# Retention heads that start their own rotary and scores early, an earlier write of token sums, and exchanged PSUM banks

## The chip, the core and the metric

The kernel runs on one core of a Trainium2 chip. A core has TensorE (PE, matmuls, with its weight loads shown as PEld), VectorE (DVE), ScalarE (ACT), GpSimd (POOL), and SyncE (SP), which here only issues transfers. Transfers between the chip's main memory (DRAM here) and on-chip SBUF run on 16 DMA engines, and are issued from the queues of SP, ACT and POOL. Matmuls write to PSUM, which has a few banks; VectorE and ScalarE read it out. The metric is the device time in microseconds (us). A comparison gives the median of several runs.

## What is computed

A trunk of two layers on 256 tokens of width 2048, in float32: gated linear attention (GLA, 4 heads), then retention (8 heads), each with a SiLU gate, and a final RMS norm. The retention layer, cut:

```python
proj = h @ w_in                               # q, k: 8 heads x 256; v, gate: 8 heads x 512
q, k = apply_rotary(q, cos, sin), apply_rotary(k, cos, sin)
scores = einsum(q, k) * dmat                  # causal, decays with a factor per head
o = scores @ v                                # (state between chunks of 64 in the reference)
o = ((o - mu) * rsqrt(var + EPS)) * gn_g + gn_b      # per head
return (o * silu(gate)) @ w_out
```

## The kernel before

Each weight matrix is read in blocks of 128 x 1024 float32 (512 KB, two slices of 128 rows by 512 columns). For each block ScalarE writes `hi` (line 283) and VectorE `lo = raw - hi` (line 284), and TensorE makes three products, hi with the high and the low part of the activations, and lo with the high part. So each block costs one ScalarE and one VectorE pass, and splits run up to three blocks ahead of TensorE (`LOOK = 3`; `hi` and `lo` have four buffers, the raw blocks eight).

For a pair of column groups (values "v" and gates "g" of a head, or two column groups of an output projection) the kernel uses products of sums of blocks (P1 to P8 in the code): some blocks are loaded a second time with an accumulating transfer on GpSimd's queue (line 292), some are added on VectorE (line 278), and the activations' token sums (`make_sums`) stand as a tensor `sums` on chip. The sums are needed again by heads 4 to 7, so `keep_sums` (line 449, GpSimd's queue) writes them to DRAM and `reload_sums` brings them back.

Order of the work: GLA heads 0 and 1, output projection "ga"; GLA heads 2 and 3, output projection "gb"; retention heads 0 to 3, output projection "ra"; heads 4 to 7, output projection "rb", and a tail. `out_pair` makes a pair of output columns: products into four banks B, A, C, V1; after the product with the fourth sum, ScalarE copies bank A to `u3`, and the blocks of `direct(lhs, (B, A), 4)` then overwrite A. `join` adds a bank into the residual on VectorE, `whole` takes its square sum on ScalarE (`sqj`).

A retention head (`ret_head`) works through a written list of tokens. Heads 1, 2, 3, 5, 6, 7 are "mixed":

```python
MIXED = "q0 q1 P1 q2 q3 q4 z P5 q5 P6 q6 q7 P2 P3 v4 v5 v6 P7 v7 g4 g5 P8 g6 g7"
```

Here q0 to q7 are the blocks of the query/key projection, P1 to P8 the products, v and g the direct blocks of values and gates. Its first half ends with q7; I call the rest, from P2, its second half. Heads 0 and 4 do all q blocks first.

The attention itself is a generator, `ret_tasks`: 1 multiply by cos (`ra`), load `dm`; 2 multiply by sin (`rb`), load `gg` and `gb`; 3 combine; 4 split into `rqs`, `rks`, score matmuls (`rs`); 5 multiply by `dm`, split scores (`rsc`); 6 output matmuls (`ro`), mean and variance; 7 multiply by `gg`; 8 the reciprocal root; 9 add `gb`; 10 multiply by the gate (`rsg`); 11 and 12 transposes (`rot_tp`) and their evacuation to `ogt`, the activations of the output projection. `step()` runs one stage. Before the change a head's stages are queued at its token P8, two run at g6 and g7, and the others in the first half of the next head; at token P2 (v5 in heads 0 and 4) what is left is run out. After heads 3 and 7, the stages run within the first blocks of "ra" and "rb" (`out_steps`), whose first two column groups leave the last two row blocks to the end (`CUT = 6`), since these need the last head's `ogt`.

A planner in the framework orders the instructions on each engine from this program; `keep` holds the written order of an engine's marked instructions, and `tc.high_priority()` lets an instruction go ahead of others. Four PSUM tiles, acc0 to acc3, serve the projections, two ("lev") hold half of q and k, two ("mis") scores, outputs and transposes. `slots` gives the order in which projections take acc0 to acc3; `acc(..., which=[n])` names one.

Of the kernel before, what the change touches and what calls it, by code (L numbers as in the profile page):

```python
# [14 lines left out]
AF = mybir.ActivationFunctionType  # L15
ALU = mybir.AluOpType

P = 128
SEQ = 256
# [142 lines left out]
def kernel(  # L162
# [17 lines left out]
    nc = tc.nc  # L180
# [20 lines left out]
    keep = tc.keep_in_program_order  # L201
# [9 lines left out]
    slots = deque(range(4))  # L211
# [4 lines left out]
    def acc(n, name, shape=(P, GW), which=None):  # L216
        out = []
        for i in range(n):
            k = slots[0] if which is None else which[i]
            if which is None:  # L220
                slots.rotate(-1)
            out.append(acc_p.tile(list(shape), F32, tag=f"acc{k}", name=f"{name}{i}"))
        return out
# [83 lines left out]
    def drain_side():  # L307
        while side:
            advance()

    def next_weights():
        i = state["sub"]
        while emitted["sub"] <= min(i + LOOK, len(subs) - 1):
            emit_split()
        state["sub"] += 1
        return splits.pop(i)
# [71 lines left out]
    def three(ps, xh, xl, hi, lo, q, stop):  # L388
        start, again = id(ps) not in begun, {"skip_group_check": id(ps) in closed}
        begun.add(id(ps))  # L390
        mm(ps, xh, hi[:, q, :], start=start, stop=False, **again)  # L391
        mm(ps, xh, lo[:, q, :], start=False, stop=False, **again)  # L392
        mm(ps, xl, hi[:, q, :], start=False, stop=stop, **again)  # L393
        if stop:
            closed.add(id(ps))

    def product(ps, left, stop=False):
        for j in range(2):
            hi, lo = next_weights()
            for q in range(SUB):  # L400
                k = j * SUB + q
                three(ps, left(k, 0), left(k, 1), hi, lo, q, stop and k == QK - 1)
# [170 lines left out]
    def square_sum(t, c):  # L573
        junk = sg_p.tile([P, GW], F32, tag="sg", name="sqj")
        nc.scalar.activation(
            junk, cur["resid"][:, t, c * GW : (c + 1) * GW], AF.Square, accum_out=ssum[:, t, c : c + 1]
        )
# [363 lines left out]
    def out_transposes(c):  # L941
        return transpose_out(
            lambda t, j: cur["resid"][:, t, c * GW + j * P : c * GW + (j + 1) * P],
            4 * c,
            S_RN + 4 * c,
            xhl,
            f"xt2_{c}",
        )

    def out_pair(c, first, name):  # L950
        lhs, s = ogt, cur["s"]
        B, A, C, V1 = acc(4, f"{name}e{c}_ps", which=list(slots))
        slots.rotate(-2)
        P5 = lev_p.tile([P, GW], F32, tag="lev", name=f"{name}e{c}_p5")
        plain = lambda kt0, t: lambda k, a: lhs[:, kt0 + k, a, t * P : (t + 1) * P]
        summed = lambda i: lambda k, a: s[i][:, k, a, :]
        u3 = t4_p.tile([P, 2, GW], F32, tag="t4", name=f"{name}e{c}_u3")[:, 0, :]

        def join(col, t, src, op=ALU.add):
            dst = cur["resid"][:, t, col * GW : (col + 1) * GW]  # L960
            if op == ALU.add:
                keep(nc.vector.tensor_tensor(dst, src, dst, ALU.add))
            else:
                keep(nc.vector.tensor_tensor(dst, dst, src, ALU.subtract))

        def whole(col, t):
            if not first:
                square_sum(t, col)

        late = deque() if first else deque([out_transposes(c)])  # L970

        def turn():
            advance()
            if late:
                next(late[0], None)

        g = c + 1
        product(A, plain(0, 0), stop=True)
        advance()
        direct(lhs, (C, V1), 4)  # L980
        join(g, 0, A)
        advance()
        product(C, summed(0))
        advance()
        direct(lhs, (C, V1), 5)
        drain_side()
        product(P5, summed(1), stop=True)
        direct(lhs, (C, V1), 6)
        for t in range(2):
            join(c, t, P5)  # L990
        product(A, summed(2), stop=True)
        product(B, plain(4, 0))
        join(c, 0, A, ALU.subtract)
        direct(lhs, (C, V1), 7, stop=True)
        product(A, summed(3), stop=True)
        join(c, 0, C)
        whole(c, 0)
        keep(nc.scalar.activation(u3, A, AF.Copy))
        direct(lhs, (B, A), 4)
        join(c, 1, u3, ALU.subtract)  # L1000
        join(c, 1, V1)
        whole(c, 1)
        direct(lhs, (B, A), 5)
        turn()
        product(A, plain(4, 1))
        turn()
        direct(lhs, (B, A), 6)
        turn()
        direct(lhs, (B, A), 7, stop=True)
        join(g, 0, B)  # L1010
        whole(g, 0)
        join(g, 1, A)
        whole(g, 1)
        if not first:
            for _ in late[0]:
                pass
            tasks.append(out_transposes(g))
        begun.clear()
        closed.clear()
# [208 lines left out]
    tasks = deque()  # L1228

    def step(n=1):  # L1230
        for _ in range(n):
            if tasks:
                try:
                    next(tasks[0])
                except StopIteration:
                    tasks.popleft()

    def ret_head(h):
        lhs = xhl
        mixed = h % 4 != 0  # L1240
        q_ps = [acc(1, f"rqk{h}_ps{c}", (P, 2, SEQ), [c + 2])[0] for c in range(2)]
        q_ps += [lev_p.tile([P, 2, SEQ], F32, tag="lev", name=f"rqk{h}_ps{c}") for c in (2, 3)]
        if not mixed:
            q_ps = q_ps[2:] + q_ps[:2]
        r, r2 = r2_[:, 0, :], r2_[:, 1, :]
        box = {}

        def qk_done():
            if h == 0:
                token_norm(r2_, "n2")  # L1250
                nc.vector.tensor_tensor(r2_[:, 1, :], r2_[:, 0, :], r2_[:, 0, :], ALU.mult)
            qk = t4_p.tile([P, 4, SEQ], F32, tag="qk", name=f"rqk{h}", bufs=1)
            tmp = t4_p.tile([P, 4, SEQ], F32, tag="t4", name=f"rqk{h}_h2")
            for c in range(4):
                nc.scalar.activation(tmp[:, c, :], q_ps[c][:, 1, :], AF.Copy)
                nc.vector.tensor_tensor(qk[:, c, :], q_ps[c][:, 0, :], tmp[:, c, :], ALU.add)
            box["qk"] = qk

        def q_step(j):
            step_w(lhs, q_ps, j)  # L1260
            if j == NSUB - 1:
                qk_done()

        def tile_of(key, pool_, shape, dtype, name):
            def get():
                if key not in box:
                    box[key] = pool_.tile(shape, dtype, tag=key, name=name)
                return box[key]

            return get  # L1270

        v = tile_of("v", v_p, [P, 2, 2, GW], F32R, f"rv{h}")
        sg = tile_of("sg", sg_p, [P, 2, GW], F32, f"rsg{h}")
        o = tile_of("o", o_p, [P, 2, GW], F32, f"re{h}")
        order = ret_order(h)
        toks = [x for x in order.split() if x != "z"]
        drain = toks.index("P2" if mixed else "v5")

        def turn(tok):
            n = toks.index(tok)  # L1280
            if n == drain:
                while tasks:
                    step()
            elif n < drain and tok not in ("q7", "P3"):
                step()
            elif tok == "P8":
                tasks.append(ret_tasks(h, box["qk"], r, r2, box))
            elif tok in ("g6", "g7"):
                step()

        def banks(n):
            if n not in box:
                box[n] = acc(1, f"re{h}_ps{n}", which=[n])[0]
            return box[n]

        values_and_gates(lhs, order, banks, v, sg, o, r, r2, turn, q_step)
# [69 lines left out]
        closed.clear()  # L1366

    def out_steps(i, j):
        step(2 if i == 0 and j < 3 else 1)

    for h in range(2):
        gla_head(h)
    slots = deque((2, 3, 0, 1))
    out_half(True, False, "ga", joint=JOINT["ao", 0])
    slots = deque((2, 3, 0, 1))
# [1 line left out]
    for h in range(2, 4):  # L1377
        gla_head(h)
    get_resid("gb_resid")
    slots = deque((0, 1, 2, 3))  # L1380
    out_half(False, False, "gb", joint=JOINT["ao", 1])
    put_resid("resid_g")
    if True:
        tasks.append(make_sums(xhl, "sums", sums_in_rs))
        for h in range(4):
            if h == 3:
                keep_sums("sums")
            ret_head(h)
    slots = deque((2, 3, 0, 1))
    tasks.append(make_sums(ogt, "rsum", sums_in_v))  # L1390
    out_half(True, False, "ra", CUT, out_steps, JOINT["ro", 0])
    put_resid("resid_r")
# [4 lines left out]
    slots = deque((2, 3, 0, 1))  # L1397
# [102 lines left out]
```

## Time and profile before

| | us |
|---|---|
| median of 3 runs | 1388.12 |
| lowest and highest | 1386.97, 1389.71 |
| the profiled execution | 1389.8 |
| its span, first to last instruction | 1387.9 |
| mean granted TensorE clock | 0.997 |

The page of the profile gives each engine's busy time and share of the span. Further views give the busy time by stretches of the span, the instructions in order of time with the idle time before each and what ended it, groups of equal instructions, and the transfers. In them L364 is line 364 of the kernel, `re_ps` a retention head's value and gate banks, `rqk_ps` its q and k, `gb_ps`, `gbe_ps`, `ra_ps`, `rb_ps` banks of the output projections. An instruction is busy from start to end; waits on semaphores are idle time.

### The profile page before, as it was taken

The page shows a single profiled execution, that of the slowest core. Times are in us where ns is not written, and L with a number is a line of the kernel's source. Part 1 is how long each engine was busy: PE and PEld are TensorE (multiplying, and loading weights), DVE is VectorE, ACT ScalarE, POOL GpSimd, SP SyncE. Part 2 cuts the span into 40 slices and gives each one's busy share as a digit, 9 for nine tenths or more (in the row PEclk, how much of TensorE's full clock was granted, in tenths as well). Part 3 has the DMA queues.
Part 4 walks back from the last instruction along what each step waited for, and adds up shares of the span by engine and source line. Part 5 has one row for each costly group of instructions (what it writes and reads, how often), then busy time and mean ns, then how long its engine had stood idle before and what let it go on. Part 6 is the DMA issues. An engine that isn't in the chain of part 4 may idle for free.

```text
span 1387.9 us, 18436 instructions
## 1 busy us (share of the span) xinstructions
PE 1370.5 (99%) x6632; PEld 1149.2 (83%) x6632; DVE 1078.2 (78%) x1497; ACT 837.4 (60%) x1104; POOL 131.9 (10%) x188
## 2 busy tenths in 40 slices
PE   9999999999999999999999999999999999999997
PEld 7888888888888888887888887887888888888887
DVE  6686795987878887779788877888767888888773
ACT  6576656655567747565666665654546666666552
POOL 1003020110021021001011010100101101010000
PEclk9999999999999999999999999999999999999999
DMA  9755556789659658758797878796698796969661
GB/s 354 247 181 167 172 170 182 165 248 349 193 152 275 184 174 219 277 166 258 227 288 200 257 228 267 197 326 201 158 377 224 235 275 174 283 174 336 205 191 62
DMA packets 83932, 312.94 MB, mean 225 GB/s; under 512 B 9713, under 2 KB 10737, under 8 KB 82561
## 3 DMA queue, kind: packets, MB, share of 16 engines
q1 hardware_dynamic: 67344, 242.64, 50.4%
q0 software_dynamic: 15056, 61.74, 22.0%
q10 hardware_dynamic: 1440, 7.38, 1.4%
q8 instruction: 52, 0.85, 0.2%
q14 instruction: 40, 0.32, 0.1%
HBM read 301.24 MB, written 10.49 MB: 225 GB/s over the span
## 4 chain that ended last, share of the span: by engine, by line
PE 51%; DMA 1%; DVE 1%; ACT 0%; issue 0%; DVEq 0%; ACTq 0%
PE rqk_ps L364 8%; PE re_ps L391 8%; PE re_ps L393 8%; PE re_ps L392 8%; PE rqk_ps L365 4%; PE rb_ps L321 2%; PE rb_ps L323 2%; PE rb_ps L322 2%; PE ra_ps L321 1%; PE ra_ps L322 1%; PE ra_ps L323 1%; PE rae_ps L392 1%; PE rae_ps L393 1%; PE rae_ps L391 1%; DMA raw<-in_w_all 1%; PE tail_ps L323 1%
## 5 line engine op out<-in xcount | busy, mean ns | idle before, releaser
L284 DVE TENSOR_TENSOR lo<-raw,hi 128x1024 fp32r<-128x1024 f32 (+1 forms) x557 | 673.7, 1221 | 231.3 <-ACT hi L283 226.2
L283 ACT ACTIVATE hi<-raw 128x1024 fp32r<-128x1024 f32 (+1 forms) x557 | 584.0, 1056 | 394.7 <-DMA raw<-in_w_all 52.5
L364 PE MATMUL rqk_ps<-xhl,hi 128*128 128x512 f32 x480 | 166.7, 397 | 0.0
L392 PE MATMUL re_ps<-lo,xhl 128*128 128x512 f32 x352 | 137.8, 391 | 0.1
L393 PE MATMUL re_ps<-hi,xhl 128*128 128x512 f32 x352 | 137.8, 392 | 0.0
L391 PE MATMUL re_ps<-hi,xhl 128*128 128x512 f32 x352 | 130.7, 392 | 0.4 <-ACT hi L283 0.4
L365 PE MATMUL rqk_ps<-xhl,lo 128*128 128x256 f32 x480 | 127.8, 281 | 0.0
L292 POOL DMA_DIRECT2D raw<-in_w_all x84 | 72.8, 868 | 570.0 <-DVE lo L284 291.3
L364 PEld LDWEIGHTS rqk_ps<-xhl,hi 128*128 128x128 f32 x480 | 89.4, 188 | 18.6
L365 PEld LDWEIGHTS rqk_ps<-xhl,lo 128*128 128x128 f32 x480 | 88.7, 189 | 3.0
L392 PEld LDWEIGHTS re_ps<-lo,xhl 128*128 128x128 f32 x352 | 66.5, 189 | 14.1 <-DVE lo L284 0.6
L391 PEld LDWEIGHTS re_ps<-hi,xhl 128*128 128x128 f32 x352 | 66.2, 188 | 14.3 <-ACT hi L283 0.8
L393 PEld LDWEIGHTS re_ps<-hi,xhl 128*128 128x128 f32 x352 | 66.4, 189 | 13.8
L364 PE MATMUL gqk_ps<-xhl,hi 128*128 128x512 f32 x216 | 76.5, 398 | 0.0
L322 PE MATMUL gg_ps<-lo,xhl 128*128 128x512 f32 x192 | 75.4, 393 | 0.0
L322 PE MATMUL gv_ps<-lo,xhl 128*128 128x512 f32 x192 | 75.2, 392 | 0.0
L321 PE MATMUL gv_ps<-hi,xhl 128*128 128x512 f32 x192 | 75.1, 393 | 0.0
L323 PE MATMUL gv_ps<-hi,xhl 128*128 128x512 f32 x192 | 75.0, 391 | 0.0
L323 PE MATMUL gg_ps<-hi,xhl 128*128 128x512 f32 x192 | 75.0, 390 | 0.0
L321 PE MATMUL gg_ps<-hi,xhl 128*128 128x512 f32 x192 | 74.8, 391 | 0.0
L365 PE MATMUL gqk_ps<-xhl,lo 128*128 128x256 f32 x216 | 59.0, 280 | 0.0
L801 POOL TENSOR_TENSOR s<-s,m 128x64 f32<-128x64 f32 x56 | 36.1, 677 | 233.4 <-DVE m L792 224.1
(407 smaller groups left out, 2683.5 us busy)
## 6 DMA issues: line engine op xcount, KB each, us to landing
raw<-in_w_all SPq DMA_DIRECT2D x451, 512.0 KB, 4.9
raw<-in_w_all POOLq DMA_DIRECT2D x84, 512.0 KB, 7.0
resid<-in_x_n SPq DMA_DIRECT2D x2, 1024.0 KB, 9.0
gg<-in_gn_g POOLq DMA_DIRECT2D x8, 256.0 KB, 5.6
resid_x<-resid ACTq DMA_DIRECT2D x1, 2048.0 KB, 8.3
gb<-in_gn_b POOLq DMA_DIRECT2D x8, 256.0 KB, 3.8
gb_resid<-resid_x POOLq DMA_DIRECT2D x1, 2048.0 KB, 11.7
resid_g<-gb_resid ACTq DMA_DIRECT2D x1, 2048.0 KB, 9.3
```

The lines of the kernel that those rows point to most:

```text
L283: a = nc.scalar.activation(hi[:, sl], src[:, sl], AF.Copy)
L284: b = nc.vector.tensor_tensor(lo[:, sl], src[:, sl], hi[:, sl].bitcast(F32), ALU.subtract)
L292: nc.gpsimd.dma_start(raws[n], block(key), accum_op=ALU.add)
L321: mm(ps, xh, hi[:, q, :], start=kt == 0, stop=False)
L322: mm(ps, xh, lo[:, q, :], start=False, stop=False)
L323: mm(ps, xl, hi[:, q, :], start=False, stop=kt == NKT - 1)
L364: mm(ps[c], wh, rhs[:, kt, :, :], start=kt == 0, stop=False)
L365: mm(ps[c][:, 0, :], wl, rhs[:, kt, 0, :], start=False, stop=False)
L391: mm(ps, xh, hi[:, q, :], start=start, stop=False, **again)
L392: mm(ps, xh, lo[:, q, :], start=False, stop=False, **again)
L393: mm(ps, xl, hi[:, q, :], start=False, stop=stop, **again)
L801: nc.gpsimd.tensor_tensor(dst, dst, side_of(m[:, li, :], z), ALU.add)
```

## The change

Four edits. In `out_pair` the copy `u3` is written ahead of the joins and marked with high priority. In `ret_head` a table `at` exchanges acc0, acc1 with acc2, acc3 in heads 0 to 3, and the `slots` of "gb" and "ra" are exchanged to match. In mixed heads the stages are queued at P2, once the tasks of the head before are run out, and one stage runs at each of P3, v4, v5, v6, v7, P8, g6 and g7; the others run in the next head's first half, where heads 0 and 4 now also run one at P3, and `out_steps` runs one a block. `keep_sums` is called ahead of head 1 in place of head 3.

```diff
@@ out_pair
         product(A, summed(3), stop=True)
+        with tc.high_priority():
+            keep(nc.scalar.activation(u3, A, AF.Copy))
         join(c, 0, C)
         whole(c, 0)
-        keep(nc.scalar.activation(u3, A, AF.Copy))
         direct(lhs, (B, A), 4)
@@ ret_head
-        q_ps = [acc(1, f"rqk{h}_ps{c}", (P, 2, SEQ), [c + 2])[0] for c in range(2)]
+        at = (2, 3, 0, 1) if h < 4 else (0, 1, 2, 3)
+        q_ps = [acc(1, f"rqk{h}_ps{c}", (P, 2, SEQ), [at[c + 2]])[0] for c in range(2)]
...
             if n == drain:
                 while tasks:
                     step()
-            elif n < drain and tok not in ("q7", "P3"):
-                step()
+                if mixed:
+                    tasks.append(ret_tasks(h, box["qk"], r, r2, box))
+            elif n < drain:
+                if tok != "q7":
+                    step()
+            elif mixed:
+                if tok not in ("P7", "g4", "g5"):
+                    step()
             elif tok == "P8":
                 tasks.append(ret_tasks(h, box["qk"], r, r2, box))
             elif tok in ("g6", "g7"):
...
-                box[n] = acc(1, f"re{h}_ps{n}", which=[n])[0]
+                box[n] = acc(1, f"re{h}_ps{n}", which=[at[n]])[0]
@@ out_steps
-        step(2 if i == 0 and j < 3 else 1)
+        step()
@@ the order of the work
-    slots = deque((0, 1, 2, 3))
+    slots = deque((2, 3, 0, 1))
     out_half(False, False, "gb", joint=JOINT["ao", 1])
...
         for h in range(4):
-            if h == 3:
+            if h == 1:
                 keep_sums("sums")
             ret_head(h)
-    slots = deque((2, 3, 0, 1))
+    slots = deque((0, 1, 2, 3))
```

## The prediction

> **What bounds the kernel now.** I read the page first (busy time by engine), then cut the span into stretches around every pause of TensorE, then compared the four retention heads that run the same program, and last looked up in the timeline what ended each pause.
>
> ```profile
> PE 1370.5 (99%) x6632; PEld 1149.2 (83%) x6632; DVE 1078.2 (78%) x1497; ACT 837.4 (60%) x1104; POOL 131.9 (10%) x188
> ```
>
> TensorE is busy for 1370.5 of 1387.9 us. The change takes no matmul away, so all it can win lies in the 17.4 us in which TensorE is idle, or in time at a lower clock. The stretches below hold (start and end:length, busy time of TensorE, weight loads, VectorE, ScalarE, GpSimd, the granted clock, the DMA engines' busy share, GB/s):
>
> ```profile
> 0.00:8.00 8.00, 4.83 (x11) 3.12 (x12) 2.57 (x5) 3.49 (x6) 2.42 (x12) 1.00 0.74 228
> 566.00:569.00 3.00, 2.54 (x12) 1.83 (x11) 2.86 (x8) 1.49 (x2) 0.00 (x0) 1.00 1.03 423
> 644.00:648.00 4.00, 2.87 (x13) 1.74 (x12) 4.00 (x5) 2.00 (x4) 0.00 (x0) 1.00 1.01 412
> 835.00:846.00 11.00, 9.32 (x35) 6.71 (x34) 6.32 (x6) 6.04 (x7) 0.00 (x0) 0.91 0.89 302
> 966.00:969.00 3.00, 1.20 (x10) 0.92 (x9) 2.71 (x5) 3.00 (x5) 0.00 (x0) 1.00 0.84 280
> 1322.00:1325.00 3.00, 2.24 (x15) 1.75 (x14) 1.62 (x2) 2.03 (x3) 0.00 (x0) 1.00 0.75 220
> 1376.00:1388.00 12.00, 3.89 (x33) 3.69 (x31) 3.64 (x12) 2.54 (x8) 0.00 (x0) 0.81 0.23 87
> ```
>
> Idle TensorE time, row by row (length less busy): 3.17 at the start, 0.46, 1.13, 1.68, 1.80, 0.76, and 8.11 at the end; together 17.11. What is left is one wait, at 323 us (a timeline row: start, duration, engine, line, what; in brackets the idle time before it and what ended that):
>
> ```profile
> 323.08 0.50 PE L392 MATMUL gae_ps<-lo,ogt 128*128 128x512 f32 x1 [0.43 <-DVE lo L284]
> ```
>
> Start and end are not touched. The five pauses in between are, and each lies at one part of the change: the entry into the output projection "gb" (567 us), the copy u3 in its column pair (645), head 2 (836 to 844), and the two waits for the last head's transposes (967 and 1323).
>
> ```profile
> 720.78:788.21 67.43, 67.43 (x337) 56.96 (x335) 55.63 (x76) 42.18 (x56) 6.90 (x9) 1.00 0.82 233
> 788.21:860.01 71.80, 70.12 (x336) 58.07 (x335) 55.91 (x76) 42.25 (x56) 7.43 (x10) 0.98 0.82 245
> 860.01:927.62 67.61, 67.61 (x336) 57.05 (x335) 55.87 (x76) 42.38 (x56) 7.49 (x10) 1.00 0.82 249
> 1148.71:1216.31 67.60, 67.60 (x336) 57.04 (x335) 56.01 (x76) 42.63 (x56) 6.91 (x9) 1.00 0.80 229
> ```
>
> These are heads 1, 2, 3 and 6, each from its first q block to the next head's. Three take 67.4 to 67.6 us with TensorE busy throughout; head 2 takes 71.80, so it loses 4.2 us: 1.68 of pause, the rest around it at a granted clock of 0.98 over the head.
>
> **The change part by part.** All sums are against the profiled execution: 1389.8 us, span 1387.9, so 1.9 us lie around the span. It is 1.7 us above the median of the three timed runs (1388.12); I carry a difference found here over to that median.
>
> *Token sums written at the second head (keep_sums at h == 1 in place of 3).* What head 2 has and the others lack is this write (its second row: KB, and us from issue to landing):
>
> ```profile
> 813.75 0.56 POOL L449 DMA_DIRECT2D sums_kept<-sums  x1
> sums_kept<-sums POOLq DMA_DIRECT2D x1, 2048.0 KB, 8.5
> 820.00:838.00 18.00, 17.87 (x90) 14.79 (x90) 13.48 (x23) 10.07 (x14) 2.27 (x3) 1.00 1.03 270
> 842.16 0.51 PE L391 MATMUL re_ps<-hi,sums 128*128 128x512 f32 x1 [1.10 <-ACT hi L283]
> 844.00:848.00 4.00, 4.00 (x12) 3.15 (x11) 3.62 (x5) 2.49 (x4) 0.00 (x0) 0.57 0.81 279
> 848.00:852.00 4.00, 4.00 (x19) 3.33 (x18) 4.00 (x6) 2.52 (x4) 0.00 (x0) 1.00 0.89 312
> ```
>
> It is issued at 813.75, just ahead of two accumulating weight loads. For 18 us after 820 the DMA engines are full (1.03); the weight tiles come late, ScalarE's split "hi" comes late, and TensorE pauses. Right behind, the clock is 0.57 for 4 us: 12 matmuls start in place of 19 (both stretches count as busy). Seven starts at 4.00/19 = 0.21 us make some 1.5 us, so pauses and clock give 3.2 of the 4.2; the rest is the slower restart after each wait. In the built order of the changed kernel the write stands on the GpSimd queue in head 0, behind the two accumulating loads of P1 and ahead of the next two (raw225, raw226). It waits only for the sums:
>
> ```profile
> 686.32 1.29 DVE L443 TENSOR_TENSOR sums<-sums_f,sums 128x512 fp32r<-128x512 f32 x2
> 686.00:690.00 4.00, 4.00 (x20) 3.30 (x19) 3.68 (x5) 3.57 (x5) 0.00 (x0) 1.00 0.04 8
> 690.00:694.00 4.00, 4.00 (x19) 3.34 (x18) 3.87 (x5) 1.77 (x3) 0.77 (x1) 1.00 0.45 133
> 693.23 0.87 POOL L292 DMA_DIRECT2D raw<-in_w_all  x1 [13.01 <-DVE raw L278]
> ```
>
> The sums are ready at 687.6 and the DMA engines are nearly idle until 690 (0.04), half idle until 694. At 8.5 us from issue to landing the write would end near 696, 3 us past the next accumulating load's issue. The bounds of the gain are 4.2 (head 2 becomes like 1, 3 and 6, no new cost) and 0 (the same collision, moved). I take 4.0, since most of the write falls into the hole, and 0.2 for the rest. [...]
>
> On the clock the rows come first: the one dip in mid-span (0.57) follows directly on a 1.10 us wait, while the 1.80 us pause at 967 left the clock at 1.00. I count the dip as caused by head 2's late loads. [...]
>
> *The u3 copy under high priority, ahead of the joins.*
>
> ```profile
> 645.93 0.63 ACT L575 ACTIVATE sqj<-gb_resid 128x512 f32<-128x512 f32 x1 [1.13 <-DVE gb_resid L962]
> 646.56 0.58 ACT L998 ACTIVATE gbe_u<-gbe_ps 128x512 f32<-128x512 f32 x1
> 646.04 0.41 PE L679 MATMUL xt_tp<-ident,gb_resid 128*128 128x128 f32 x2 [0.39 <-DVE gb_resid L962]
> 647.19 0.50 PE L391 MATMUL gbe_ps<-hi,ogt 128*128 128x512 f32 x1 [0.74 <-ACT gbe_u L998]
> ```
>
> ScalarE stands idle for 1.13 us in front of the square sum, which waits for VectorE's join; u3 is queued behind it, and TensorE waits for u3 before it may overwrite bank A. In the changed order u3 stands ahead of split 251 and the square sum, so it can run in that idle 1.13 us; the transposes that waited 0.39 stand later on TensorE. Queued behind u3's own wait (for product A) are only split 251 and the square sum, neither due sooner. So 1.13 at most. What is late next is VectorE: the stretch from 644 to 648 has it busy for 4.00 of 4.00. I take 0.8, between 0 and 1.13. In the other three pairs the only pause is the 0.43 at 323 us, for a split: nothing.
>
> *PSUM banks exchanged.*
>
> ```profile
> 567.93 0.47 PE L321 MATMUL gb_ps<-hi,ogt 128*128 128x512 f32 x1 [0.46 <-DVE hr_nw L476]
> ```
>
> The first gb group used banks 0 and 1, the gate banks of the group before, which are read out last; it now uses 2 and 3, the value banks, read out earlier. Gain 0.46 (0 to 0.46). Heads 0 to 3 and "ra" are relabelled together, and before head 4 there was no pause to win: 0.
>
> *Mixed heads start their tasks in their own second half.* Eight of a head's steps (rotary, scores, output product) leave the next head's first half, so at the end of heads 3 and 7 five steps are left in place of twelve.
>
> ```profile
> 968.61 0.50 PE L321 MATMUL ra_ps<-hi,ogt 128*128 128x512 f32 x1 [1.80 <-ACT ogt L686]
> 1323.89 0.50 PE L321 MATMUL rb_ps<-hi,ogt 128*128 128x512 f32 x1 [0.76 <-ACT ogt L686]
> ```
>
> Both waits are for ogt, the evacuation of the last head's transposes. In the changed order these stand some five 12-matmul blocks ahead of the first use in ra, seven in rb, where now they stand right in front of it. Gain 1.80 + 0.76 = 2.56 (0 only if the transposes are not moved). One step a block in out_steps in place of two is enough: five tasks and six steps of "rsum" fit the twelve early blocks.
>
> The price lies in the second halves, on VectorE. A second half in the trace, and what is added to it or taken from it (groups: count | busy us, mean ns of one | idle before):
>
> ```profile
> 1185.00:1216.30 31.30, 31.30 (x143) 25.96 (x142) 26.02 (x30) 19.24 (x22) 2.24 (x3) 1.00 0.90 282
> L1154 DVE TENSOR_TENSOR ra<-rqk,trig 128x1024 f32<-128x1024 f32 x3 | 3.7, 1218 | 0.0
> L1154 DVE TENSOR_TENSOR ro<-ro,rsg 128x512 f32<-128x512 f32 x4 | 2.7, 682 | 0.0
> L1154 DVE TENSOR_TENSOR ra<-ra,rb 128x512 f32<-128x512 f32 x4 | 2.6, 685 | 0.0
> L1154 DVE TENSOR_TENSOR rb<-rqk,trig 128x512 f32<-128x512 f32 x4 | 2.6, 684 | 0.0
> L687 DVE TENSOR_TENSOR ogt<-rot_tp,ogt 128x512 fp32r<-128x512 f32 x4 | 2.6, 680 | 0.0
> L1154 DVE TENSOR_TENSOR rqs<-ra,rqs 128x512 fp32r<-128x512 f32 x2 | 1.4, 686 | 0.0
> L1154 DVE TENSOR_TENSOR rs<-rs,dm 128x384 f32<-128x384 f32 x2 | 1.1, 549 | 0.0
> ```
>
> Added up to the score split: 1.22 + 2 x 0.68 + 2 x 0.69 + 0.69 for rqs, at most the same for the smaller rks, and 2 x 0.55 for the scores and their split: 6.4 us. Gone to the first half: 2 x 0.68 + 2 x 0.68 = 2.7. So 26.0 + 6.4 - 2.7 = 29.7 of VectorE in 31.3 us of TensorE, which itself grows by the moved score and output matmuls. That fits, at 95% or less; in heads 1 and 5, where the previous head's tail still stays in the second half, nothing is taken away: 32.4, about equal to the longer half. VectorE's new wait (the score multiply, for the score matmuls of v7) has the splits of P8 queued behind it, but the value sums ahead of it wait for v7 already. On the GpSimd queue dm and gg move ahead of accumulating loads; their buffers are free by then in the built order (gb's last reader stands ahead of P6's split), so they hold nothing up. I put 0.3 us on the whole, between 0 and 2 us for each of six heads, the size of the largest pause seen.
>
> Sum: 4.0 + 0.8 + 0.46 + 2.56 - 0.3 = 7.5 us; a slow restart came with each pause too (the matmul after it takes 0.47 to 0.51 us), some 0.1 each at the four smaller ones: 7.9. The profiled execution would be 1381.9, the median 1388.12 - 7.9 = 1380.2 us.
>
> **The rivals.** *The collision moves.* The write is late or slow, P5 to P7 of head 0 starve as head 2 did, and 4.0 to 4.2 us are lost again there. For it: accumulating loads follow at 693.23 and share the engines. Against: the 0.04 and 0.45 of DMA share. Time: 1380.2 + 4.1 = 1384.3. [...]
>
> *The dip of the clock stays.* It has another cause than the late loads and comes again at full cost, 1.5 us; for it, the longer pause at 967 had none. Time: 1381.7. [...]
>
> *VectorE becomes the bound of the second halves (slower).* The split of a weight tile comes late behind the eight steps, once in each of six mixed heads. It decides from where the added work no longer fits, 31.3 us against 29.7; with a pause of 2 us a head (1.80 is the largest seen) it costs 12 us: 1380.2 + 12 = 1392. Against: 26.0 us busy now, and matmuls that move along.
>
> *Little is won.* The pauses are refilled by later ones since VectorE (78%) and the weight loads (0.8 to 0.9 of DMA share in the heads) have no room to run ahead; 1.5 us a head in four heads takes 6.0 of the 7.9: 1386.2, inside 0.2% (2.8 us), which is about what a measurement of this kernel can tell from no change.
>
> **How the numbers follow.** My forecast has 0.68, the dip that stays 0.04, the moved collision 0.14, little won 0.06, VectorE-bound 0.08. Faster: 0.86; same: 0.06; slower: 0.08. The range reaches down to all five pauses gone with nothing paid (4.2 + 1.13 + 0.46 + 2.56 + 0.5 = 8.85) with the fastest run of the three as its base (1386.97 - 8.85 = 1378.1, rounded to 1378.0), and up to the moved collision with 0.3 more for the splits, 1384.6.
>
> **What would show it.** Right: head 2 as long as head 3; no TensorE pause over 0.5 us at gb's entry, at u3, at the ends of heads 3 and 7; the granted clock at 1.00 in mid-span; sums_kept landing by 696. Wrong: pauses on hi or lo in head 0 after 690 (the collision moved), or on lo in P8 to g7 of heads 1, 2, 5 and 6 (VectorE-bound).

## The result, and the profile after

| | before | after |
|---|---|---|
| median of 6 runs, us | 1388.9 | 1379.8 |
| lowest to highest | 1386.97 to 1389.71 | 1378.94 to 1382.26 |
| profiled execution, us | 1389.8 | 1379.47 |
| its span | 1387.9 | 1377.6 |

The ratio after to before is 0.9939, with a 95% interval from 0.9926 to 0.9952: 6.7 to 10.3 us less, 8.5 in the middle (the two medians lie 9.1 apart). The forecast was 7.9 us less, at 1380.2.

From the page of the changed kernel, the span, the busy time by engine and the chain of waits by engine:

```profile
span 1377.6 us, 18438 instructions
PE 1366.5 (99%) x6632; PEld 1148.5 (83%) x6632; DVE 1079.1 (78%) x1497; ACT 836.0 (61%) x1104; POOL 131.8 (10%) x188
PE 99%; DMA 0%; DVE 0%; ACT 0%; DVEq 0%; issue 0%; SPq 0%
```

TensorE's idle time fell from 17.4 to 11.1 us (span less busy time), and its busy time by 4.0, with the same 6632 matmuls. The chain that ended last is TensorE from end to end. The stretches below hold the places of the five pauses (columns as in the prediction; the first and the last row are the start and the end of the span):

```profile
0.00:8.00 8.00, 4.88 (x11) 3.17 (x12) 2.53 (x5) 3.15 (x5) 2.41 (x12) 1.00 0.73 231
560.00:570.00 10.00, 10.00 (x46) 8.29 (x45) 8.90 (x22) 6.95 (x10) 0.00 (x0) 1.00 1.01 414
640.00:650.00 10.00, 10.00 (x46) 7.96 (x45) 8.55 (x9) 7.35 (x9) 0.00 (x0) 1.00 0.98 380
786.00:856.00 70.00, 70.00 (x347) 58.79 (x346) 56.17 (x76) 43.78 (x62) 6.93 (x9) 1.00 0.80 222
955.00:965.00 10.00, 10.00 (x46) 8.29 (x45) 5.23 (x6) 3.50 (x4) 0.00 (x0) 1.00 0.65 203
1318.00:1326.00 8.00, 8.00 (x37) 6.61 (x36) 7.07 (x9) 4.56 (x8) 0.54 (x1) 1.00 0.66 209
1366.00:1377.60 11.60, 3.57 (x30) 3.37 (x29) 3.64 (x12) 2.55 (x8) 0.00 (x0) 0.82 0.24 90
```

In every row between the start and the end the second number equals the first: TensorE has no pause left at gb's entry, at u3, in head 2, or in front of ra's and rb's last blocks. What is left is 3.12 us at the start and 8.03 at the end, 11.15 together, which is all of its idle time. In mid-span the granted clock is 1.00, head 2's place included.

What moved can be seen on ScalarE and GpSimd (timeline rows of the changed kernel; the fourth is the first matmul that needs the activations of the third):

```profile
642.27 0.57 ACT L997 ACTIVATE gbe_u<-gbe_ps 128x512 f32<-128x512 f32 x1
684.82 0.56 POOL L449 DMA_DIRECT2D sums_kept<-sums  x1 [7.64 <-DVE sums L443]
946.40 1.09 ACT L686 ACTIVATE ogt<-rot_tp 128x512 fp32r<-128x512 f32 x2 [0.18 <-PE rot_tp L679]
959.49 0.39 PE L321 MATMUL ra_ps<-hi,ogt 128*128 128x512 f32 x1
```

The copy u3 stands ahead of the square sum (which starts at 644.44), with no wait in front of it. ogt's evacuation ends at 947.5, twelve microseconds before its first use, where before it stood right in front of it. The write of the sums is issued at 684.82, as soon as the sums are ready; what it meets is shown by its row among the transfers (KB, us from issue to landing) and then by four stretches:

```profile
sums_kept<-sums POOLq DMA_DIRECT2D x1, 2048.0 KB, 9.5
```

```profile
684.00:688.00 4.00, 4.00 (x20) 3.30 (x19) 3.69 (x4) 3.28 (x4) 0.56 (x1) 1.00 0.64 262
688.00:692.00 4.00, 4.00 (x19) 3.34 (x18) 4.00 (x5) 1.64 (x3) 0.86 (x1) 1.00 0.93 293
692.00:696.00 4.00, 4.00 (x20) 3.30 (x19) 3.47 (x3) 2.88 (x4) 2.56 (x3) 1.00 1.04 267
700.00:710.00 10.00, 10.00 (x46) 8.28 (x45) 7.76 (x8) 5.24 (x8) 0.00 (x0) 1.00 1.04 304
```

It lands at 694.3. Everything ahead of it runs 3 us earlier than before: the sums are ready at 684.5, where they were at 687.6. So most of the write falls into the stretch that before had a share of 0.04 and 0.45, and its last 3 us lie behind it. The engines are full from 692 on (1.04), as they were in head 2 of the kernel before, but no split comes so late that TensorE stops.

The time thus came from two sources in the trace: 6.3 us of idle TensorE in mid-span, and 4.0 us of slow busy time (the half-clock stretch, and the restarts after each pause, both measured below). Their 10.3 us are more than the 8.5 of the comparison; a reason is found below.

### The profile page after: what moved, and what is told of

Same layout as the page of the kernel before. It is cut to its first block, busy times and chain, and to the rows that moved or that the text cites. A ratio compares the mean times of both kernels' runs of the same rounds, so it can differ in the third digit from the quotient of the medians.

```text
span 1377.6 us, 18438 instructions
## 1 busy us (share of the span) xinstructions
PE 1366.5 (99%) x6632; PEld 1148.5 (83%) x6632; DVE 1079.1 (78%) x1497; ACT 836.0 (61%) x1104; POOL 131.8 (10%) x188
## 4 chain that ended last, share of the span: by engine, by line
PE 99%; DMA 0%; DVE 0%; ACT 0%; DVEq 0%; issue 0%; SPq 0%
PE rqk_ps L364 8%; PE re_ps L392 8%; PE re_ps L391 8%; PE re_ps L393 8%; PE rqk_ps L365 4%; PE gqk_ps L364 4%; PE gg_ps L322 3%; PE gv_ps L321 3%; PE gv_ps L322 3%; PE gv_ps L323 3%; PE gg_ps L323 3%; PE gg_ps L321 3%; PE ge_ps L392 2%; PE ge_ps L393 2%; PE ge_ps L391 2%; PE gae_ps L391 2%
## 5 line engine op out<-in xcount | busy, mean ns | idle before, releaser
L364 PE MATMUL rqk_ps<-xhl,hi 128*128 128x512 f32 x480 | 162.8, 397 | 0.0
L365 PE MATMUL rqk_ps<-xhl,lo 128*128 128x256 f32 x480 | 122.3, 280 | 0.0
```

The source lines that it names most:

```text
L364: mm(ps[c], wh, rhs[:, kt, :, :], start=kt == 0, stop=False)
L365: mm(ps[c][:, 0, :], wl, rhs[:, kt, 0, :], start=False, stop=False)
```

## The experiments

Four kernels take one part of the change each, four undo one part each, one doubles the moved write, one puts it at another head, and two repeat profiles for the clock. The theory was the prediction's: each pause has its own cause in one of the edits, and the write costs nothing as long as it lies in the hole after head 0's sums. The rival was that pauses only move.

**One part alone.** *The write alone:*

```diff
-            if h == 3:
+            if h == 1:
                 keep_sums("sums")
```

> The kernel before with keep_sums at head 1 in place of head 3, nothing else. Theory (the write collided with head 2's loads, and the hole in head 0 hides it): head 2 falls from 71.8 to about 67.6 us, no dip of the clock in mid-span, head 0 unchanged, the total about 4 us less (0.3%). Rival (the collision moves): head 0 is about 4 us longer and the total the same. Rival (the dip of the clock has another cause): head 2 loses its pauses, but some stretch of 3 to 4 us still runs at half clock, the total about 2.5 us less.

Measured: ratio 0.9979 (0.9971 to 0.9988), 2.9 us less; span 1385.7. Head 2 is mended, with full clock (first row), yet TensorE slows down at another place: behind the wait for ogt at ra, which in the kernel before had left the clock at full (the stretches first, then the timeline row of that wait).

```profile
788.21:855.83 67.62, 67.62 (x336) 57.04 (x335) 55.81 (x76) 42.54 (x56) 6.89 (x9) 1.00 0.81 228
966.00:970.00 4.00, 4.00 (x12) 3.15 (x12) 0.54 (x1) 0.00 (x0) 0.00 (x0) 0.62 0.27 103
```

```profile
964.45 0.50 PE L321 MATMUL ra_ps<-hi,ogt 128*128 128x512 f32 x1 [1.79 <-ACT ogt L686]
```

So the pauses of head 2 do belong to the write, but the dip does not.

*The tasks alone* (the two hunks of `ret_head`'s task list, and `out_steps`):

```diff
+                if mixed:
+                    tasks.append(ret_tasks(h, box["qk"], r, r2, box))
...
-        step(2 if i == 0 and j < 3 else 1)
+        step()
```

> The kernel before with the mixed heads' stages begun in their own second half and one stage a block in out_steps, nothing else. Theory: the waits for ogt (1.80 at 967, 0.76 at 1323) go, 2.6 to 3 us; and keep_sums, written as before ahead of head 3, is issued later than before, in head 3's first half, where the moved stages have changed the load: if the collision depends on where the write meets the accumulating loads, head 2 loses its 4.2 us and head 3 may gain some of it. So 3 to 7 us less in total. Rival (VectorE becomes the bound of second halves): pauses on lo in P8 to g7 of heads 1, 2, 5, 6, heads 5 and 6 longer than 67.6 by up to 2 us each, total as before or longer.

Measured: 0.9981 (0.9972 to 0.9990), 2.6 us less; span 1382.9. Both waits for ogt are gone. The planner then moved the write of the sums, still called at head 3, from head 2 into head 3, and it paused TensorE there instead (0.86 at 883.9). Pauses of 0.18 and 0.75 on `lo` came at 922 and 924, which further runs show not to be the write's. There was no dip in mid-span, and with 3.5 us its idle time in mid-span is the least of the four (4.9 with the write alone, 5.3 with u3, 5.8 with the banks), so its span is the shortest.

*u3 alone:*

```diff
+        with tc.high_priority():
+            keep(nc.scalar.activation(u3, A, AF.Copy))
         join(c, 0, C)
         whole(c, 0)
-        keep(nc.scalar.activation(u3, A, AF.Copy))
```

> The kernel before with the copy u3 ahead of the joins under high priority, nothing else. Theory: the pause at 645 (0.39 and 0.74) goes, and with VectorE full there 0.8 to 1.5 us less in total; all other pauses stay. Rival (VectorE is late next): the same time comes back as waits on lo within the next four blocks, total within 0.3 us of before.

Measured: 0.9987 (0.9977 to 0.9996), 1.8 us less; span 1385.6. The two waits at u3 are gone. Head 2's pauses were smaller in this execution (0.23 and 0.53), without a dip.

*The banks alone:*

```diff
+        at = (2, 3, 0, 1) if h < 4 else (0, 1, 2, 3)
...
-    slots = deque((0, 1, 2, 3))
+    slots = deque((2, 3, 0, 1))
     out_half(False, False, "gb", joint=JOINT["ao", 1])
...
```

> The kernel before with the PSUM banks exchanged, nothing else. Theory: the pause at gb's entry (0.46 at 567) goes, 0.5 to 0.6 us less; all other pauses stay, and nothing changes before head 4. Rival: the wait only moves to the first split of gb, total unchanged.

Measured: 0.9998 (0.9987 to 1.0009), no difference that shows; span 1386.9. The 0.46 us at gb's entry is gone from the trace (its stretch follows; the kernel before had 2.54 busy in it), too little for the interval of 1.5 us to each side.

```profile
566.00:569.00 3.00, 3.00 (x15) 2.47 (x14) 2.86 (x10) 2.25 (x3) 0.00 (x0) 1.00 1.03 421
```

The four add up to 7.6 us (2.9 + 2.6 + 1.8 + 0.3), against 8.5 for the whole.

**One part undone** in the changed kernel, to compare with 0.9939. *The write back at head 3:*

```diff
-            if h == 1:
+            if h == 3:
                 keep_sums("sums")
```

> The changed kernel with keep_sums back ahead of head 3, all else changed; its write then stands between the two accumulating loads of P1 in head 3. Theory (the write costs where it meets the loads of a head's middle, and nothing in head 0's hole): head 3 is 1.5 to 2.5 us longer than heads 2 and 6, with pauses on hi or lo, and head 0 keeps its length; total 2 to 4 us more than the changed kernel, the upper end if the clock dips at those pauses. Rival (head 0 paid for the write in the changed kernel): head 0 gets shorter by what head 3 gets longer, total as the changed kernel.

Measured: 0.9962 (0.9949 to 0.9974), 3.2 us more than the changed kernel, with intervals that just overlap. The write now stands in head 3 between two accumulating loads (the timeline, GpSimd's rows and then TensorE's), and TensorE waits for the splits behind it (0.48 us at 879.37 and the fourth row):

```profile
860.69 0.89 POOL L292 DMA_DIRECT2D raw<-in_w_all  x1 [1.25 <-DVE rh_nw L471]
861.25 0.90 POOL L449 DMA_DIRECT2D sums_kept<-sums  x1
863.03 0.87 POOL L292 DMA_DIRECT2D raw<-in_w_all  x1 [0.88 <-DVE rh_nw L475]
882.84 0.74 PE L365 MATMUL rqk_ps<-xhl,lo 128*128 128x256 f32 x4 [0.91 <-DVE lo L284]
923.93 0.50 PE L392 MATMUL re_ps<-lo,xhl 128*128 128x512 f32 x1 [0.74 <-DVE lo L284]
```

Just before the fourth row the splits got nothing, as one stretch shows: VectorE does 0.65 us of work and ScalarE none, with the DMA engines at 1.05. The last row, with 0.31 more at 921.5, is not the write's: the same two pauses come back below with u3 undone, where the write stands in head 0. So the trace gives the write 1.39 us of pause, and not all of the 3.2.

```profile
872.00:876.00 4.00, 4.00 (x28) 3.61 (x28) 0.65 (x1) 0.00 (x0) 0.00 (x0) 1.00 1.05 306
```

*The tasks back:*

```diff
-                if mixed:
-                    tasks.append(ret_tasks(h, box["qk"], r, r2, box))
...
-        step()
+        step(2 if i == 0 and j < 3 else 1)
```

> The changed kernel with the stages of mixed heads queued at P8 again and two stages a block in out_steps, all else changed. Theory: the two waits for ogt are back (1.80 and 0.76), nothing else; 2.7 to 3.2 us more than the changed kernel. On the clock: if a dip of one window comes with any pause of about 1.8 us that fills enough of a window, the total may be another 1.7 us more in some executions; if the dip needs late loads as in head 2, the clock stays at full speed in mid-span. Rival (moved stages cost VectorE time in the second halves): heads 5 and 6 get shorter by some tenths, and the total rises by less than 2.5 us.

Measured: 0.9971 (0.9960 to 0.9982), 4.4 us more. Both waits are back at their old size (timeline), and the clock stays at full behind the longer one (the first stretch):

```profile
963.86 0.50 PE L321 MATMUL ra_ps<-hi,ogt 128*128 128x512 f32 x1 [1.79 <-ACT ogt L686]
1319.44 0.53 PE L321 MATMUL rb_ps<-hi,ogt 128*128 128x512 f32 x1 [0.76 <-ACT ogt L686]
```

```profile
966.00:970.00 4.00, 4.00 (x19) 3.33 (x18) 1.12 (x1) 1.06 (x1) 0.00 (x0) 1.00 0.14 57
317.00:333.00 16.00, 14.51 (x61) 10.90 (x60) 11.09 (x12) 11.49 (x15) 0.00 (x0) 1.00 0.92 321
```

The last row is the output projection "ga". Of the edits only u3's reaches it, and this kernel has that edit as the changed kernel has. It lost 1.5 us here; with the banks undone 1.6; in the kernel before 0.43; in the changed kernel none (16.00 of 16.00 between 316 and 332). So single executions differ by one or two microseconds where the code is the same. The profiled execution of the kernel before lies 0.9 above its median and that of the changed kernel 0.3 below, which is 1.2 of the 1.8 between 10.3 and 8.5.

*u3 back behind the joins:*

```diff
-        with tc.high_priority():
-            keep(nc.scalar.activation(u3, A, AF.Copy))
         join(c, 0, C)
         whole(c, 0)
+        keep(nc.scalar.activation(u3, A, AF.Copy))
```

> The changed kernel with the copy u3 behind the joins again, all else changed. Theory (the pause belongs to the order of u3 on ScalarE, whatever happens elsewhere): the pause of 0.4 and 0.7 us at u3 in gb is back, no other in the heads; 1.0 to 1.6 us more than the changed kernel. Rival (the single edit's 1.8 us came from a softer collision in head 2, not from u3): the pause is back but the total is within 0.5 us of the changed kernel, since VectorE was the next bound there.

Measured: 0.9962 (0.9949 to 0.9975), 3.2 us more, with intervals that just overlap. The two waits are back, in their old order:

```profile
646.31 0.41 PE L679 MATMUL xt_tp<-ident,gb_resid 128*128 128x128 f32 x2 [0.40 <-DVE gb_resid L962]
647.45 0.50 PE L391 MATMUL gbe_ps<-hi,ogt 128*128 128x512 f32 x1 [0.74 <-ACT gbe_u L998]
```

That is 1.1 us; beside it this execution had 0.96 in "ga", 0.49 on `lo` at 644.5, 0.31 and 0.75 on `lo` at 921 and 923, and 0.51 on `hi` at 1122.5. The two at 921 and 923 lie at the end of head 3's second half, where VectorE has no idle time for 20 us:

```profile
908.00:928.00 20.00, 18.94 (x87) 15.14 (x87) 20.00 (x25) 12.15 (x15) 1.11 (x2) 1.00 0.85 304
```

The tasks alone and the write undone have the same two pauses at the same place; the changed kernel and the other undone ones have none. Why they come in some kernels and not in others is not settled.

*The banks back:*

```diff
-    slots = deque((2, 3, 0, 1))
+    slots = deque((0, 1, 2, 3))
     out_half(False, False, "gb", joint=JOINT["ao", 1])
...
```

> The changed kernel with the PSUM banks of before, all else changed. Theory: the pause at gb's entry is back (0.46 at 567), 0.5 to 0.7 us more than the changed kernel, and no other pause. Rival (the exchange is worth nothing, as the single edit's time says): the pause is back, but the time is won again before the end of gb, total within 0.3 us of the changed kernel; heads and projections as long as there.

Measured: 0.9951 (0.9939 to 0.9963), 1.7 us more, with intervals that overlap. The pause at gb's entry is back at 0.45:

```profile
570.14 0.47 PE L321 MATMUL gb_ps<-hi,ogt 128*128 128x512 f32 x1 [0.45 <-DVE hr_nw L476]
```

The four undone parts add up to 12.5 us (3.2 + 4.4 + 3.2 + 1.7), well over the 8.5 of the whole, where the four alone gave 7.6. Each undone kernel also stopped at places that its edit does not reach (1.5 and 1.6 us in "ga", 1.06 at the end of head 3), and each figure has an interval of 1.7 us or so to each side. So what one part is worth is known to a microsecond or two, not better.

**How much the hole holds.** The sums are written twice in head 0; nothing reads the second copy:

```diff
         keep(nc.gpsimd.dma_start(kept, cur["s_whole"].rearrange("p i k a t -> p (i k a t)")))
+        again = dram_p.tile([P, 4 * QK * 2 * P], F32R, tag=name + "2", name=f"{name}_again")
+        keep(nc.gpsimd.dma_start(again, cur["s_whole"].rearrange("p i k a t -> p (i k a t)")))
```

> The changed kernel with the token sums written twice in a row in head 0, to two places; the second copy is not read. Theory (the hole in the DMA engines' load near 686 to 694 us hides the first write): the second write does not fit, the accumulating loads for P7 and P8 wait 5 us longer, and head 0 gets pauses of 1 to 4 us on hi or lo. Rival (head 0 has slack for any write, no hole is needed): no pause, head 0 as long as in the changed kernel.

Measured: 0.9982 (0.9973 to 0.9990), 6 us more than the changed kernel. The first copy lands in 9.1 us, the second in 14.6, and TensorE runs for only half of the six microseconds from 704 on, waiting for ScalarE's splits (the transfers, a stretch, the timeline):

```profile
sums_kept<-sums POOLq DMA_DIRECT2D x1, 2048.0 KB, 9.1
sums_again<-sums POOLq DMA_DIRECT2D x1, 2048.0 KB, 14.6
```

```profile
704.00:710.00 6.00, 2.90 (x9) 1.57 (x10) 2.65 (x3) 3.17 (x4) 0.00 (x0) 1.00 1.06 274
```

```profile
704.72 0.51 PE L391 MATMUL re_ps<-hi,sums 128*128 128x512 f32 x1 [1.03 <-ACT hi L283]
708.60 0.50 PE L391 MATMUL re_ps<-hi,sums 128*128 128x512 f32 x1 [1.19 <-ACT hi L283]
```

So head 0 has room for one write at this place, not for two.

**Is head 0 the only place?** My next theory was that a write in the first half of a mixed head always costs 2 to 4 us. The changed kernel with the write at head 2:

```diff
-            if h == 1:
+            if h == 2:
                 keep_sums("sums")
```

> The changed kernel with keep_sums ahead of head 2; its write then stands between the two accumulating loads of P1 in head 2. Theory (a 2 MB write in a mixed head's first half meets that head's accumulating loads): head 2 and the start of its second half lose 2 to 4 us in pauses on hi or lo, as head 3 does with the write at its place, total 2 to 4 us more than the changed kernel. Rival (head 3 suffered for the transfers next to it at its own end, the residual's and those of ra): no pause in head 2, total as the changed kernel.

Measured: 0.9942 (0.9929 to 0.9955), the same as the changed kernel. The theory fell. The write was issued at 791.03, landed after 10.9 us, and head 2 shows no pause (a timeline row and two stretches):

```profile
796.84 0.88 POOL L292 DMA_DIRECT2D raw<-in_w_all  x1 [4.92 <-DVE lo L284]
```

```profile
788.00:856.00 68.00, 68.00 (x338) 57.35 (x338) 55.36 (x75) 42.23 (x58) 7.50 (x10) 1.00 0.85 253
808.00:812.00 4.00, 4.00 (x21) 3.37 (x20) 3.93 (x8) 2.96 (x4) 0.00 (x0) 1.00 0.09 37
```

The second accumulating load follows only at 796.84, where in head 3 it followed 1.8 us behind the write, and the engines are idle again by 808 (0.09). That fits a theory of queue order. A second difference lies in the loads: in the changed kernel, without a write there, the DMA engines have time to spare soon after the place of the write in head 2 (first row), and in head 3 they are full from 864 to 872 (second row; the next four microseconds have 0.09):

```profile
792.00:796.00 4.00, 4.00 (x26) 3.55 (x25) 2.59 (x5) 3.90 (x8) 0.87 (x1) 1.00 0.43 84
868.00:872.00 4.00, 4.00 (x26) 3.53 (x25) 3.58 (x5) 1.59 (x2) 0.00 (x0) 1.00 1.01 360
```

No run separated the two, so why head 3 pays and head 2 doesn't stays open. But head 2 had no stretch near zero like head 0's and still hid the write, so such a stretch was enough here and not needed.

**What the dip of the clock hangs on.** Twelve profiles had shown three dips, at different places. In the records of the clock, the dip of the kernel before is one stretch of 3.41 us at half speed, with full speed on both sides:

```profile
840.70:844.12 3.42, 1.87 (x7) 1.05 (x6) 1.98 (x2) 3.07 (x4) 0.00 (x0) 1.00 0.72 295
844.12:847.53 3.41, 3.41 (x9) 2.67 (x8) 3.25 (x4) 2.37 (x3) 0.00 (x0) 0.50 0.81 287
847.53:850.95 3.42, 3.42 (x17) 2.81 (x15) 3.20 (x5) 2.40 (x3) 0.00 (x0) 1.00 0.90 313
```

It starts 832.85 us after the first record of full clock (at 11.27 us of the span), which is 244.0 times its own 3.413 us. In the changed kernel the half clock behind the last matmul starts 1361.92 us after that first record (at 11.56 us), 399.0 times 3.413 us. So in these two traces the changes lie on a grid of 3.41 us. The further stretches are cut in the same way, in each execution from its own first full clock. The first row above, with head 2's pauses, is the stretch ahead of the dip. Ahead of the other two dips lie one of the kernel with the banks alone, in head 2 as well,

```profile
838.67:842.09 3.42, 1.79 (x7) 1.12 (x7) 2.07 (x2) 3.16 (x4) 0.00 (x0) 1.00 0.71 289
```

and one of the kernel with the write alone, at the wait for ogt:

```profile
962.21:965.62 3.41, 1.62 (x10) 1.22 (x8) 3.12 (x5) 2.68 (x5) 0.00 (x0) 1.00 0.76 222
```

Two with about as little busy time were followed by none, of the kernel before at its wait for ogt, and of the double write:

```profile
967.00:970.41 3.41, 1.80 (x8) 1.49 (x9) 3.34 (x5) 2.05 (x5) 0.00 (x0) 1.00 0.70 209
```

```profile
705.78:709.19 3.41, 1.94 (x6) 1.05 (x6) 0.75 (x2) 1.70 (x2) 0.00 (x0) 1.00 1.07 275
```

TensorE's busy time does not separate them (1.87 with a dip, 1.80 without). Two of the kernels were profiled once more, unchanged:

> The kernel before, unchanged, profiled once more, to see what the half-clock dip hangs on. Theory W (a window on a fixed grid): the records of the clock change only on a grid of 3.41 us that starts with the first full clock (at 9 to 12 us of the span, another place in every execution). [...] Theory L (the prediction's: the dip belongs to head 2's late loads): a dip at 842 to 848 us again, wherever the grid lies, and none near 967. Spans: 1387.9 with one dip, about 1386.3 with none, 1389.5 with two.

Measured: span 1387.6 and no dip, neither in head 2 nor near 967 (the clock is 1.00 from 788 to 1030). Head 2's pauses were 0.52, 0.56 and 0.44 this time.

```profile
840.00:844.00 4.00, 3.00 (x13) 1.92 (x12) 2.48 (x3) 3.57 (x4) 0.00 (x0) 1.00 0.75 272
844.00:848.00 4.00, 4.00 (x19) 3.33 (x18) 4.00 (x5) 2.49 (x4) 0.00 (x0) 1.00 0.92 288
```

So the dip does not come with head 2's late loads each time. The span was expected at 1386.3 without a dip. Pauses of 0.46 at 1007 and 0.28 at 1071, which the first profile didn't have, account for most of the 1.3 us between: idle time in mid-span is 0.35 longer, and two more restarts cost 0.3 each (worked out below). The rest, some 0.35 us, is not accounted for.

> The kernel before with the earlier write alone, profiled once more. In its first profile a dip followed the 1.79 us wait near 964 us, which lay wholly in one grid window. [...] Theory L in its weaker form (with head 2 mended, the dip belongs to the wait at the entry of ra): a dip at 964 to 969 us again, whatever the grid, and a span of 1385.7.

Measured: span 1384.4, no dip. The wait is again 1.79 us long, but a border of the grid cuts it, 1.44 us in front of the border (first row, length less busy) and the rest behind:

```profile
960.23:963.64 3.41, 1.97 (x13) 1.50 (x11) 3.12 (x5) 2.79 (x5) 0.00 (x0) 1.00 0.89 279
964.00:968.00 4.00, 4.00 (x18) 3.33 (x19) 2.08 (x4) 0.50 (x2) 0.00 (x0) 1.00 0.53 155
```

Same kernel, nearly the same idle time (4.94 and 4.90 us in mid-span), spans of 1385.7 and 1384.4: in this pair the dip is worth 1.3 us. It came where the wait lay within one stretch (962.66 to 964.45, in the row of 962.21 to 965.62), and not where a border cut it. Both repeats were without a dip, so that the place on the grid decides is the author's estimate from this pair, and no run has shown it.

## Why the prediction came out

**Five pauses, each with its own edit: right.** All five are gone, each came back when its edit was undone (the write's in head 3, not in head 2), and each had gone when its edit was made alone.

**The write of the sums, 4.0 us: the mechanism right, the size a mixture.** Measured 2.9 alone and 3.2 undone. It landed at 694.3, inside the forecast of 696, but only because the sums were ready 3 us earlier: from there it took 9.8 us, against 8.4 forecast. Most of it lay in the hole that the rows 0.04 and 0.45 showed; doubled, it cost 6 us. The rival that the collision moves was thus near: one more write of that size would have made it true.

**The failed step: "I count the dip as caused by head 2's late loads".** The write alone mended head 2 and left a dip at ra; the kernel before ran once more without any. The 1.5 us of dip in the 4.0 belong to no edit. The dips seen followed pauses at two places, head 2 and ra's wait, and the same places had pauses without one (head 2's 0.52, 0.56 and 0.44 us in the second profile of the kernel before, and its 1.80 at 967 in the first); what decides is not shown. In the changed kernel, where mid-span has no pause, the clock stayed at 1.00. The sum survived because both places were mended together.

**u3, 0.8 us: too low.** The whole 1.13 went: VectorE, taken to be late next, was not, with 8.55 of 10 us busy after. Measured 1.8 alone and 3.2 undone, each with an interval of more than a microsecond to each side and the latter with pauses elsewhere.

**Banks, 0.46: right in the trace** (0.46 and 0.45); too small for the times.

**Tasks, 2.56 less 0.3: the gain right, the price paid in some kernels only.** Both waits went, with ogt ready 12 us early; measured 2.6 alone and 4.4 undone. The second halves of heads 3 and 6, in stretches of the same length as the one shown before:

```profile
889.99:921.29 31.30, 31.30 (x144) 26.05 (x143) 29.00 (x36) 18.94 (x22) 2.71 (x4) 1.00 0.93 295
1176.70:1208.00 31.30, 31.30 (x144) 26.06 (x143) 27.09 (x32) 18.84 (x23) 2.22 (x3) 1.00 0.83 246
```

VectorE went from 26.02 to 27.09 in head 6, where 29.7 was forecast, and stands at 29.00 in head 3, and TensorE does not stop. The rival of a bound there, priced at 12 us, did not come in the changed kernel. But three other kernels with this edit paid 0.9 to 1.06 us at the end of head 3 (the pauses on `lo` near 923, VectorE busy throughout), so the price of 0.3 was not empty.

**Restarts, 0.4 us: mis-sized.** TensorE's busy time fell by 4.0 us. Less the 1.5 for the dip, 2.5 are left for nine pauses, 0.3 each and not 0.1. The starts of the matmuls show the same. Around the wait at 323 us (0.43 idle) they start at 322.26, 323.08 and 323.42, so 1.16 us pass where two starts in a full stretch take 0.45: 0.3 more than the idle time, since a stop loses the overlap of matmuls that take 0.39 and start 0.227 apart (850.95 to 852.99 us, nine starts on), and the first one after it takes 0.50. Added up over the nine pauses it is 2.5. The forecast had 0.1 at the four smaller pauses, and 1.0 for three pauses in its sum for head 2, which is 0.3 each already.

**The total, 7.9 us: inside the interval, with luck in it.** The terms were read from one profiled execution, and between the two profiled ones the difference is 10.3: u3 and the restarts were put too low, and the wait at 323 went too, though no edit was credited with it. The comparison gave 8.5 partly because the profiled execution of the kernel before lay 0.9 above its median. The forecast median came within 0.4 us of the measured one because its base, 1388.12, was also 0.8 below the later median. The rival that little is won did not come: in mid-span TensorE no longer stops.

## What to carry to other kernels

Compare twin sections of a kernel: one that is longer than its likes names its cause by what it has and they lack, and a transfer that waits for nothing can go where the DMA share is near zero (here 0.04 and 0.45 over 8 us), if its length fits there (one write of 9.5 us cost no pause, two cost 6 us; other places may do as well, as head 2 did). Price a half-clock stretch to the pauses around it as a chance and not to one cause, and expect that it may reappear at another pause (here at 966 us, 0.62, once head 2 was mended). And where a kernel waits in few places, part-by-part gains add up only roughly: a planner may move a transfer when another edit is made, as the tasks alone did with the write.

## What the runs showed of the hardware

In mid-span the clock fell to half in three of the 14 profiles: in the kernel before from 844.12 to 847.53 us (0.50 for 3.41 us), with the banks alone (0.57 between 842 and 846) and with the write alone (0.62 between 966 and 970). In the dip of the kernel before, matmuls of 512 columns start 0.43 us apart (844.14, 844.56, 844.99), and 0.227 apart at 850.95 to 852.99. In the 3.41 or 3.42 us ahead of the three dips TensorE was busy for 1.87, 1.79 and 1.62 us. Stretches of 3.41 us with 1.80 (the kernel before, 967), 1.94 (the double write) and 1.97 (the write alone, once more) were followed by full clock. The longest pause that a dip followed was 1.79 us (the write alone), and one of 1.80 was followed by none (the kernel before, 967). Which pauses a dip follows, these runs do not settle.
